# A two-block network in one program: modulation dot products of 1024 rows, all of the first layer's in the first block, loaded from a queue and a pool of their own

## The chip, the core and the metric

One core of a Trainium2 chip runs one program. TensorE (PE in the profile, its weight loads PEld) multiplies matrices, VectorE (DVE) and ScalarE (ACT) work elementwise, GpSimd (POOL) does small chores and issues some DMAs, SyncE (SP) issues most DMAs. Each engine runs its own list of instructions in the order written and waits at semaphores. The metric is the device time of one execution in microseconds (us), median of several runs.

## The reference

Two networks follow each other. The first is one block on a 256 x 2048 input: a norm, a projection to 12288 columns, three branches (multi-window pooling, a 31-tap causal convolution with a layer norm, a short gated convolution), gates, an output projection, and a gated feed-forward layer with a 3-tap convolution. The second has two layers with three kinds of attention over 256 latent and 256 context tokens, and each layer is modulated by a vector:

```
shift, scale, gate       = split(silu(c)     @ w_ada[l] + b_ada[l], 3)
shift_c, scale_c, gate_c = split(silu(c_ctx) @ w_ada[l] + b_ada[l], 3)
h  = rms(x,  norm_w[l]) * (1 + scale)   + shift
hc = rms(xc, norm_w[l]) * (1 + scale_c) + shift_c
...
x  = x + gate * merge_out(...)
xc = xc + gate_c * merge_out(...)      # not in the last layer
```

`w_ada[l]` is 2048 x 6144. Shift and scale are needed where a layer begins, the gates only at its output projection.

## The kernel before

**Weights.** Every product of two f32 matrices is done in three matmuls on split operands (high x high, high x low, low x high). A weight chunk of eight 128 x 128 tiles (512 KB) is loaded by SP into `raw`, ACT rounds it to `wh` (L187), DVE subtracts to get `wl` (L188), and PE runs 24 matmuls of 256 columns on it (L215, L216 on `wh`, then L218 on `wl`). `raw`, `wh` and `wl` have three buffers each, so PE stalls when ACT or DVE falls more than that behind. `w` (L178) records these steps at a priority 400 instructions ahead.

**Order.** A scheduling layer takes the recorded instructions by priority and readiness and writes each engine's list; a list is then fixed. The names in the trace follow the program: `xs`, `hid`, `xsc` are split inputs, `mm` and `st` are PSUM banks.

**Modulation.** It is done on DVE beside the weights, not on PE. For each group of 128 output columns (48 groups) and each of the two vectors, one dot instruction (L400) multiplies a `rawm` tile (128 columns x 512 rows of `w_ada`, transposed) with `crow` (the vector's 512 values, broadcast to all partitions), and accumulates into `mod`. Four passes over 512 rows give 48 x 2 x 4 = 384 dots for the first layer; the second needs 320, since its context gates are unused. One `rawm` load (512 KB) holds two groups, so four dots. `rawm` has two buffers in the weights' pool, and the load for the next four dots is recorded just before the present four. Before each load POOL copies one element (`mark`, L386) that depends on the newest `wl`, so that the load is not issued long before its turn; SP issues the load (L387).

**When.** The dots are tasks with a cost. `earn` (L198) credits the time of the matmuls just recorded times a rate, and runs tasks while there is credit; `spend` takes away other DVE work. The rate is 0.88 in the first block; 0.53, 0.45 and 0.4 in the first layer of the second block; 0.3, 0.3 and 0.5 in the second. In the first block the tasks of the 31-tap convolution come first (`urgent`), then shift and scale of the first layer (256 dots), then its gates (128 dots), as far as the credit goes; what is left of the gates goes on in the second block, before the second layer's dots. At output 8 of the 16 of the last projection (`fdn`, weights `raw<-in_fdn`, L630 to L649) shift and scale must be complete, and from there `ctx_in` (L693) runs: it loads the context in four pieces `xc` into the `rawm` buffers, sums squares (`acc`, L345), makes the norm, loads the pieces again, and makes `xsc` by 16 `h` (L690) and 16 splits (L352). The second block's first products (the `z` gates, weights `in_wz`) read `xsc`. `lat_in` (L715) then stores the four pieces of `x` (`xo<-x`, POOL) and makes `xl`. `norm_conv` (L652) normalises the convolution in four steps at outputs 2, 4, 6 and 7 of the gate loop.

Of the kernel before, what the change touches and what calls it, by code (L numbers as in the profile page):

```python
# [8 lines left out]
F32 = mybir.dt.float32  # L9
# [12 lines left out]
RATES = ((0.53, 0.45, 0.4), (0.3, 0.3, 0.5))  # L22
T = 256
D = 2048
# [50 lines left out]
def lay_out(i):  # L75
# [23 lines left out]
    o["wada"] = two(lambda l: i["w_ada_2"][l].reshape(4, 512, 24, 2, 128).transpose(2, 0, 4, 3, 1))  # L99
# [53 lines left out]
class Net:  # L153
    def __init__(self, tc, aps):
        self.tc, self.nc, self.a = tc, tc.nc, aps
        self.tasks, self.urgent = [], []
        self.credit, self.rate = 0.0, 0.0
        self.ahead = 400
# [131 lines left out]
    def small(self, n, name, bufs=2):  # L290
        return self.st.tile([128, n], F32, name=name, tag=f"s_{name}{n}", bufs=bufs)
# [77 lines left out]


    def modulation(self, l, parts, last):

        nc = self.nc
        mod = self.cr.tile([128, 2, 48], F32, name="mod", tag=f"mod{l}", bufs=1)
        crow, raws = [None], []

        def rows(q):
            c = self.cr.tile([128, 2, 512], F32, name="crow", tag="crow", bufs=1)
            src = self.silu
            nc.sync.dma_start(c, bass.AP(tensor=src.tensor, offset=src.offset + q * 512,  # L380
                                         ap=[[0, 128], [D, 2], [1, 512]]))
# [8 lines left out]
        def pair(q, j, follow):  # L390
            if follow:
                load(*follow)
            raw = raws.pop(0)
            for s in range(2):
                for v in range(2):
                    if last and v and 2 * j + s >= 32:
                        continue
                    junk = self.cr.tile([128, 512], BF16, name="junk", tag="junk", bufs=1)
                    m = mod[:, v, 2 * j + s:2 * j + s + 1]
                    nc.vector.tensor_tensor_reduce(  # L400
                        out=junk, in0=raw[:, s * 512:(s + 1) * 512], in1=crow[0][:, v], op0=OP.mult, op1=OP.add,
                        scale=1.0, scalar=self.col("bada", 2 * j + s, l) if q == 0 else m, accum_out=m)

        lists = []
        for js in ((0, 16), (16, 24)):
            order = [(q, j) for q in range(4) for j in range(*js)]
            tasks = [(0.0, lambda at=order[0]: load(*at))]
            for (q, j), follow in zip(order, order[1:] + [None]):
                if j == js[0]:
                    tasks.append((0.0, lambda q=q: rows(q)))  # L410
                tasks.append((1.4 if last and j >= 16 else 2.7, lambda q=q, j=j, follow=follow: pair(q, j, follow)))
            lists.append(tasks)
        return mod, lists
# [11 lines left out]
    def block1(self):  # L425
# [50 lines left out]
        for j in range(8):  # L476
            pv = proj_in(8 + j)
            pg = proj_in(16 + j)
            if j == 0:
                acc = self.tmp(name="acc")  # L480
                for k in range(16):
                    self.sumsq(acc, x[k], k == 0)
                R = self.rnorm_rows(acc, D, "R1")
                nc.gpsimd.tensor_copy(self.vec2[:, 0, :1], self.mark)
                nc.scalar.dma_start(self.vec2, a["vec2"].rearrange("l p c -> p l c"))
                nc.scalar.dma_start(self.icnt, a["icnt"].rearrange("p (g c) -> p g c", g=4))
                self.silu_rows()
                self.rate = 0.88
# [17 lines left out]
        pooled = self.big.tile([128, 4096], F32, name="pooled", tag="slot", bufs=5)[:, :12 * (8 + T)]  # L506
        pooled = pooled.rearrange("p (b j t) -> p b j t", b=6, j=2)
        nc.gpsimd.memset(pooled[:, :, :, :8], 0.0)
        for g in range(4):
# [7 lines left out]
            for _ in range(g + 1):  # L517
# [5 lines left out]
                                    in1=self.icnt[:, g, None, :w - 1].to_broadcast([128, 2, w - 1]), op=OP.mult)  # L523
# [28 lines left out]
        for f in range(16):  # L552
# [10 lines left out]
            if f in (2, 4, 6, 7):  # L563
                next(norm, None)
                self.spend(4)
# [66 lines left out]
        for f in range(16):  # L632
# [19 lines left out]
    def norm_conv(self, v, c):  # L652

        nc = self.nc
        lsum = self.tmp()
        nc.vector.tensor_reduce(lsum, c.rearrange("p k t -> p t k"), axis=AX.X, op=OP.add)
# [5 lines left out]
        nc.vector.tensor_tensor(out=c, in0=c, in1=mean[:, None, :].to_broadcast([128, 8, T]), op=OP.subtract)  # L662
        nc.scalar.activation(v, c, AF.Square)
        nc.vector.tensor_reduce(lsum, v.rearrange("p k t -> p t k"), axis=AX.X, op=OP.add)
        yield
        r = self.rnorm(lsum, 1024)
        yield
        RL = self.to_rows(r, "RL")
        nc.vector.tensor_tensor(out=c, in0=c, in1=RL[:, None, :].to_broadcast([128, 8, T]), op=OP.mult)
# [23 lines left out]
    def ctx_in(self, xsc):  # L693
# [3 lines left out]
        def piece(q):  # L697
            t = self.wp.tile([128, 1024], F32, name="xc", tag="rawm", bufs=2).rearrange("p (k t) -> p k t", t=T)
# [394 lines left out]
    def proj_c(self, l):  # L1093
# [14 lines left out]
        for name, j0, n, vec, nt in (("ckv", 6, 4, "kvan", 4), ("cq", 0, 6, "qan", nq)):  # L1108
            acc = self.tmp(512, "acc")
            tiles = []  # L1110
            for j in range(n):
                ps = self.bank()
                for k0 in (0, 8):
# [10 lines left out]
                    self.earn(1.28 * nt)  # L1124
# [358 lines left out]
    def modulation_tasks(self, l):  # L1483
        self.mod[l], lists = self.modulation(l, None, l == 1)
        return lists


def net_kernel(tc, aps, stage=2):
# [5 lines left out]
    with contextlib.ExitStack() as es:  # L1494
# [9 lines left out]
        n.cr.tile([128, 16], F32, name="pad", tag="pad")  # L1504
# [11 lines left out]
        n.icnt = n.px.tile([128, 4, 16], F32, name="icnt")  # L1516
        with contextlib.ExitStack() as e2:
            n.big, n.sm, n.ht = (pool(e2, x, side="right") for x in ("big", "sm1", "ht"))
# [4 lines left out]
            n.left = len(deferred)  # L1523
            n.tasks += deferred
            x, acc, n.xc = n.block1()
        n.xlp, n.sm = (pool(es, x, **right) for x in ("xl", "sm2"))
# [35 lines left out]
```

## Time and profile before

| | us |
|---|---|
| median of 3 runs (lowest, highest) | 3245.82 (3238.53, 3248.12) |
| the profiled execution | 3237.02 |
| its span, first to last instruction | 3235.2 |
| PE busy | 3144.7 (97%) |
| DVE busy | 2493.5 (77%) |
| ACT busy | 1541.8 (48%) |
| POOL busy | 131.1 (4%) |

A busy share is a mean over the whole span. PE's is near the whole, so what another engine does counts only where PE waits for it. An engine's idle time is charged to what ended it.

### The profile page before, as it was taken

How to read it: one execution, taken by the hardware profiler on the slowest of the kernel's cores; microseconds unless marked ns; L12 is line 12 of the kernel's file. 1: busy time of each engine (PE TensorE's matmuls, PEld its weight loads, DVE VectorE, ACT ScalarE, POOL GpSimd, SP SyncE). 2: the span in 40 equal slices, each digit the busy share in tenths (PEclk: the TensorE clock that was granted, in tenths of full speed). 3: DMA queues.
4: the chain of work that ended last, by engine and by line, in shares of the span. 5: the costliest groups of instructions: out<-in, count | busy, mean ns of one | idle time of the engine just before them, and what ended most of it. 6: DMA issues, size and time to landing. Idle time of an engine off the chain costs nothing. (4 is left out here: it accounts for less than half of the span.)

```text
span 3235.2 us, 64395 instructions
## 1 busy us (share of the span) xinstructions
PE 3144.7 (97%) x25390; PEld 3097.1 (96%) x25390; DVE 2493.5 (77%) x5285; ACT 1541.8 (48%) x2579; POOL 131.1 (4%) x328
## 2 busy tenths in 40 slices
PE   8999999999999999989999999999999999999999
PEld 8999999999999999989999999999999999999999
DVE  8889977877888888767677888789768776764764
ACT  5444444444554555435444545335545453553553
POOL 0000000000000000000000000000011001000010
PEclk9999999999999999999999999999999999999999
DMA  6556666666666666777654445555477755443456
GB/s 215 182 184 196 205 225 218 225 223 218 218 222 202 228 214 219 232 225 244 186 166 156 140 136 184 190 169 168 154 221 260 229 180 183 136 132 119 128 181 196
DMA packets 190079, 623.16 MB, mean 193 GB/s; under 512 B 21936, under 2 KB 33936, under 8 KB 189776
## 3 DMA queue, kind: packets, MB, share of 16 engines
q1 hardware_dynamic: 180896, 591.75, 56.2%
q0 software_dynamic: 8176, 26.78, 2.5%
q8 instruction: 199, 3.26, 0.4%
q14 instruction: 104, 0.85, 0.1%
q10 hardware_dynamic: 704, 0.52, 0.1%
HBM read 600.33 MB, written 18.63 MB: 191 GB/s over the span
## 5 line engine op out<-in xcount | busy, mean ns | idle before, releaser
L187 ACT ACTIVATE wh<-raw 128x1024 fp32r<-128x1024 f32 (+4 forms) x930 | 940.0, 1013 | 1012.9 <-PE mm L216 283.6
L188 DVE TENSOR_TENSOR wl<-raw,wh 128x1024 fp32r<-128x1024 f32 (+4 forms) x930 | 1081.5, 1164 | 336.5 <-ACT wh L187 320.5
L215 PE MATMUL mm<-xs,wh 128*128 128x256 f32 x2912 | 698.7, 281 | 10.1 <-ACT wh L187 9.8
L216 PE MATMUL mm<-xs,wh 128*128 128x256 f32 x2912 | 697.8, 280 | 2.1 <-DVE xs L355 2.1
L215 PEld LDWEIGHTS mm<-xs,wh 128*128 128x128 f32 x2912 | 550.9, 189 | 11.0 <-ACT wh L187 10.5
L216 PEld LDWEIGHTS mm<-xs,wh 128*128 128x128 f32 x2912 | 551.2, 189 | 2.9 <-DVE xs L355 2.9
L400 DVE CUSTOM_DVE_ANT_0 junk<-rawm,crow,mod 128x512 bf16<-128x512 f32 x528 | 395.5, 749 | 163.9 <-DMA rawm<-in_wada 128.3
L218 PE MATMUL mm<-xs,wl 128*128 128x256 f32 x2912 | 400.3, 280 | 11.9 <-DVE wl L188 11.9
L218 PEld LDWEIGHTS mm<-xs,wl 128*128 128x128 f32 x2912 | 366.0, 189 | 14.1 <-DVE wl L188 13.9
L215 PE MATMUL mm<-hid,wh 128*128 128x256 f32 x688 | 168.1, 284 | 3.4 <-ACT wh L187 3.3
L224 PE MATMUL mm<-wh,xl 128*128 128x384 f32 (+3 forms) x512 | 168.9, 336 | 0.0
L216 PE MATMUL mm<-hid,wh 128*128 128x256 f32 x688 | 167.4, 283 | 0.0
L400 DVE CUSTOM_DVE_ANT_0 junk<-rawm,crow,vec 128x512 bf16<-128x512 f32 x176 | 131.8, 749 | 43.0 <-DMA rawm<-in_wada 40.6
L225 PE MATMUL mm<-wh,xl 128*128 128x384 f32 (+3 forms) x512 | 164.5, 327 | 0.0
L1122 PE MATMUL mm<-xl,wh 128*128 128x256 f32 x640 | 147.6, 279 | 0.0
L215 PEld LDWEIGHTS mm<-hid,wh 128*128 128x128 f32 x688 | 132.8, 193 | 4.2 <-ACT wh L187 4.2
L216 PEld LDWEIGHTS mm<-hid,wh 128*128 128x128 f32 x688 | 133.0, 193 | 0.0
L386 POOL COPY rawm<-wl 128x1 f32<-128x1 f32 x192 | 51.2, 268 | 1944.9 <-DVE wl L188 1534.9
L215 PE MATMUL mm<-xl,wh 128*128 128x256 f32 x512 | 126.2, 286 | 0.0
L215 PE MATMUL mm<-ys,wh 128*128 128x256 f32 x512 | 123.8, 285 | 0.0
L227 PE MATMUL mm<-wl,xl 128*128 128x384 f32 (+3 forms) x512 | 123.4, 327 | 0.0
L216 PE MATMUL mm<-xl,wh 128*128 128x256 f32 x512 | 122.9, 280 | 0.0
(370 smaller groups left out, 6879.6 us busy)
## 6 DMA issues: line engine op xcount, KB each, us to landing
raw<-in_w1in SPq DMA_DIRECT2D x192, 512.0 KB, 4.2
rawm<-in_wada SPq DMA_DIRECT2D x192, 512.0 KB, 5.0
raw<-in_fup SPq DMA_DIRECT2D x172, 512.0 KB, 4.5
raw<-in_wz SPq DMA_DIRECT2D x96, 512.0 KB, 4.1
raw<-in_wout SPq DMA_DIRECT2D x96, 512.0 KB, 4.8
raw<-in_fdn SPq DMA_DIRECT2D x80, 512.0 KB, 4.6
raw<-in_proj SPq DMA_DIRECT2D x48, 512.0 KB, 4.2
raw<-in_wcq SPq DMA_DIRECT2D x40, 512.0 KB, 4.0
```

What stands on the lines that cost most here:

```text
L187: nc.scalar.activation(wh, raw, AF.Copy)
L188: nc.vector.tensor_tensor(out=wl, in0=raw, in1=wh.bitcast(F32), op=OP.subtract)
L215: mm(ps, wh, h, start=first and i == 0, stop=False)
L216: mm(ps, wh, l, start=False, stop=False)
L218: mm(ps, wl, h, start=False, stop=last and i == len(parts) - 1)
L224: mm(ps, h, wh, start=first and i == 0, stop=False)
L225: mm(ps, l, wh, start=False, stop=False)
L227: mm(ps, h, wl, start=False, stop=last and i == len(parts) - 1)
L386: nc.gpsimd.tensor_copy(raw[:, :1], self.mark)
L400: nc.vector.tensor_tensor_reduce(out=junk, in0=raw[:, s * 512:(s + 1) * 512], in1=crow[0][:, v], op0=OP.mult, op1=OP.add, scale=1.0, scala ...
L1122: nc.tensor.matmul(ps[:, s * T:(s + 1) * T], wp, x, start=first and s == 0, stop=k == 15 and m == 2, skip_group_check=True)
```

## The change

- `w_ada` is laid out for dots of up to 1024 rows. The pool for `rawm`, `crow` and `junk` is now its own: 1024 wide in the first block (two `rawm` buffers), 512 wide in the second (four). One `rawm` load of 512 KB holds one group of 1024 rows, so two dots; in the second block a load of 256 KB holds one group of 512 rows, two dots.
- All 192 dots of the first layer (96 groups and passes, two vectors) are tasks of the first block; `later` at output 8 of `fdn` runs all that are left. The second block has the second layer's 320 dots of 512 rows alone.
- The loads of `rawm` and `crow` are issued by POOL, not SP. POOL's `mark` copy stands only before the first loads of a list; later loads wait for their buffer alone. The next load is recorded after the dots.
- Rates are 0.84, 0.36 and 0.3/0.3/0.5. A task of 6.0 us that does nothing stands behind each `crow` load. `proj_c` earns nothing after its last output.
- `ctx_in` takes its `xc` pieces from the new pool's `rawm` buffers.
- `norm_conv` adds by a tree of three adds, works in halves, and is spread over outputs 3 to 8. `icnt` moves into an unused end of a tile, small tiles of `rsqrt` share three buffers, and a pad grows from 16 to 64.

```
-RATES = ((0.53, 0.45, 0.4), (0.3, 0.3, 0.5))
+RATES = ((0.36, 0.36, 0.36), (0.3, 0.3, 0.5))
...
+    def mod_tile(self, name):
+        return self.mp.tile([128, self.wide], F32, name=name, tag="rawm", bufs=8192 // (4 * self.wide))
...
         def rows(q):
-            c = self.cr.tile([128, 2, 512], F32, name="crow", tag="crow", bufs=1)
+            c = mp.tile([128, 2, wide], F32, name="crow", tag="crow", bufs=1)
...
-            nc.sync.dma_start(c, ...
+            nc.gpsimd.dma_start(c, ...
...
-        def load(q, j):
-            raw = self.wp.tile([128, 1024], F32, name="rawm", tag="rawm", bufs=2)
-            nc.gpsimd.tensor_copy(raw[:, :1], self.mark)
-            nc.sync.dma_start(raw.rearrange("p (k c) -> p k c", c=512), self.a["wada"][l, j, q])
+        def load(q, f, wait=False):
+            raw = self.mod_tile("rawm")
+            if wait:
+                nc.gpsimd.tensor_copy(raw[:, :1], self.mark)
+            at = q * wide % 1024
+            nc.gpsimd.dma_start(raw, self.a["wada"][l, q * wide // 1024, f][:, at:at + wide])
...
+        lists, ahead = [], 2048 // wide - 1
+        for fs in ((0, 32), (32, 48)):
+            order = [(q, f) for q in range(D // wide) for f in range(*fs)]
+            tasks = [(0.0, lambda at=at: load(*at, wait=True)) for at in order[:ahead]]
+            for (q, f), follow in zip(order, order[ahead:] + [None] * ahead):
+                if f == fs[0]:
+                    tasks += [(0.0, lambda q=q: rows(q)), (6.0, lambda: None)]
+                cost = (0.23 + wide / 960) * (1 if last and f >= 32 else 2)
+                tasks.append((cost, lambda q=q, f=f, follow=follow: dots(q, f, follow)))
...
             if f == 8:
-                self.later(len(self.tasks) - self.left)
+                self.later(len(self.tasks))
...
-            t = self.wp.tile([128, 1024], F32, name="xc", tag="rawm", bufs=2).rearrange("p (k t) -> p k t", t=T)
+            t = self.mod_tile("xc").rearrange("p (k t) -> p k t", t=T)
...
-                    self.earn(1.28 * nt)
+                    if j < n - 1:
+                        self.earn(1.28 * nt)
```

The first place is DVE's list in the gate loop of the first block, some 480 us in (`gate`, `m` and `brb` belong to that loop, `junk` is a dot's unused product, a row `mod` reads the sum). Before:

```order
L188 TENSOR_TENSOR wl<-raw,wh 128x1024
L400 ISA junk,mod<-rawm,crow,mod 128x512
L400 ISA mod 128x1
L400 ISA junk,mod<-rawm,crow,mod 128x512
L400 ISA mod 128x1
L591 TENSOR_TENSOR gate<-mm,gate 128x256
L188 TENSOR_TENSOR wl<-raw,wh 128x1024
```

And now:

```order
L189 TENSOR_TENSOR wl<-raw,wh 128x1024
L361 TENSOR_TENSOR brb<-tmp,brb 128x256
L403 ISA junk,mod<-rawm,crow,vec_81 128x1024
L403 ISA mod 128x1
L189 TENSOR_TENSOR wl<-raw,wh 128x1024
L467 TENSOR_TENSOR gate<-mm,R_344 128x256
L403 ISA junk,mod<-rawm,crow,vec_81 128x1024
L403 ISA mod 128x1
L189 TENSOR_TENSOR wl<-raw,wh 128x1024
```

A wide dot now stands behind nearly every `wl`. Before, 114 dots of 512 rows stand between the 135th and the 260th of the 930 `wl`; now 127 dots of 1024 rows stand there, one more up to the 507th, and 49 from there to the 548th, which is the last `wl` of `fdn`.

The second place is DVE's list around the context's norm and `xsc`. Before, it stands between the `wl` of `fdn`'s outputs 10 to 13:

```order
L188 TENSOR_TENSOR wl<-raw,wh 128x1024
L345 TENSOR_TENSOR acc<-acc,sq 128x256 x2
L690 SCALAR_TENSOR_TENSOR h<-xc,gain,Rc 128x256 x3
L188 TENSOR_TENSOR wl<-raw,wh 128x1024
L352 SCALAR_TENSOR_TENSOR xsc<-h,mod,xsc 128x256 x3
L690 SCALAR_TENSOR_TENSOR h<-xc,gain,Rc 128x256
L188 TENSOR_TENSOR wl<-raw,wh 128x1024
```

Now the end of the last dots and the beginning of the context's sums read:

```order
L403 ISA junk,mod<-rawm,crow,mod 128x1024
L403 ISA mod 128x1
L348 TENSOR_TENSOR acc<-acc,sq 128x256 x19
L303 TENSOR_SCALAR rsv<-st 128x2
L348 TENSOR_TENSOR acc<-acc,sq 128x256
```

These rows stand behind the last `wl` of `fdn`, behind the three `wl` of the next products, and behind the addition of `fdn`'s last output to `x`. Between that addition and the sums stand 12 dots, and the next `wl` comes after 12 of the 16 `h` and 8 of the 16 `xsc`.

The third place is POOL's list, with what each row waits for (PE and Activation stand for semaphores of those engines, DVE for VectorE's, DMASW for a DMA that POOL issued), near the end of the first layer's loads. Now:

```order
L395 DMA rawm<-in_wada 128x1024 [waits DMASW0_49,DVE_49]
L386 DMA crow<-silu 128x2x512 [waits PE_49,Activation_49]
L395 DMA rawm<-in_wada 128x1024 [waits DMASW1_49,DVE_49]
L395 DMA rawm<-in_wada 128x1024 [waits DMASW2_49,DVE_49]
L755 DMA xo<-x 128x1024 [waits DMAHW0_49,DVE_49]
L395 DMA rawm<-in_wada 128x1024 [waits DMASW4_49,DVE_49]
L395 DMA rawm<-in_wada 128x1024 [waits DMASW5_49,DVE_49]
L395 DMA rawm<-in_wada 128x1024 [waits DMASW7_49,DVE_49]
L395 DMA rawm<-in_wada 128x1024 [waits DMASW0_49,DVE_49]
```

The row `crow` of 2 x 512 is the second layer's first one. It is written where a `hid` tile of the first block lies, and the PE semaphore that it waits for is that of the last matmul of `fdn` on that tile. Six of the first layer's loads stand behind it. Before, POOL's list there held only `mark` copies, `xo` and `bias`.

## Rows read from the trace of the kernel before

**Rows 1.** The page, part 1: busy us, share, count.

```profile
PE 3144.7 (97%) x25390; PEld 3097.1 (96%) x25390; DVE 2493.5 (77%) x5285; ACT 1541.8 (48%) x2579; POOL 131.1 (4%) x328
```

**Rows 2.** Waits of PE, whole span: total us, times, longest.

```profile
PE mm L218 <- DVE wl L188: 26.0, 22, 3.4
```

**Rows 3.** Waits of DVE, whole span.

```profile
DVE junk L400 <- DMA rawm<-in_wada: 169.0, 106, 4.8
DVE junk L400 <- DMA crow<-silu: 21.5, 7, 5.8
```

**Rows 4.** Timeline of DVE near 1378 us: start, us, instruction, idle before it.

```profile
1377.30 0.75 DVE L400 CUSTOM_DVE_ANT_0 junk<-rawm,crow,vec 128x512 bf16<-128x512 f32 x1 [2.75 <-DMA rawm<-in_wada]
...
1380.37 2.35 DVE L188 TENSOR_TENSOR wl<-raw,wh 128x1024 fp32r<-128x1024 f32 x2
```

**Rows 5.** Stretches: length; PE, PEld, DVE, ACT, POOL busy (count); clock; DMA.

```profile
376.00:742.00 366.00, 352.47 (x2997) 349.03 (x2997) 288.40 (x517) 169.48 (x216) 6.64 (x27) 1.00 0.66 221
742.00:1450.00 708.00, 690.72 (x5826) 687.20 (x5826) 576.97 (x1042) 341.24 (x463) 14.64 (x50) 0.99 0.66 219
1450.00:1560.00 110.00, 106.79 (x914) 106.00 (x914) 78.04 (x137) 59.32 (x91) 1.05 (x2) 0.98 0.74 237
...
1625.00:2033.00 408.00, 399.47 (x2825) 388.30 (x2824) 335.49 (x912) 201.36 (x488) 27.80 (x69) 1.00 0.49 158
2033.00:2283.00 250.00, 241.11 (x1951) 235.80 (x1950) 209.59 (x537) 100.90 (x185) 10.77 (x36) 0.99 0.55 175
...
2571.00:2694.00 123.00, 117.48 (x810) 115.04 (x809) 92.11 (x236) 56.62 (x113) 7.47 (x23) 0.99 0.57 185
2694.00:3235.20 541.20, 529.49 (x4159) 513.74 (x4157) 334.08 (x834) 261.30 (x511) 27.77 (x55) 0.99 0.48 154
```

**Rows 6.** The dots of L400 alone in such stretches: DVE busy (two instructions each).

```profile
376.00:742.00 366.00, 86.35 (x228) 1.00 0.66 221
...
1450.00:1560.00 110.00, 3.51 (x10) 0.98 0.74 237
1625.00:2033.00 408.00, 147.38 (x390) 1.00 0.49 158
2033.00:2283.00 250.00, 97.59 (x257) 0.99 0.55 175
2571.00:2694.00 123.00, 21.20 (x56) 0.99 0.57 185
```

**Rows 7.** DVE by form, whole span: count, busy us, mean ns, idle before.

```profile
L188 DVE TENSOR_TENSOR wl<-raw,wh 128x1024 fp32r<-128x1024 f32 x776 | 947.6, 1222 | 265.7 <-ACT wh L187 254.1 <-PE at L364 5.7 <-PE mm L218 1.5
...
L345 DVE TENSOR_TENSOR acc<-acc,sq 128x256 f32<-128x256 f32 x105 | 42.7, 420 | 3.5 <-ACT sq L344 2.3
...
L352 DVE SCALAR_TENSOR_TENSOR xsc<-h,mod,xsc 128x256 fp32r<-128x256 f32 x16 | 7.0, 478 | 0.0
L690 DVE SCALAR_TENSOR_TENSOR h<-xc,gain,Rc 128x256 f32<-128x256 f32 x16 | 6.9, 478 | 0.0
```

**Rows 8.** Windows at DVE's densest and in PE's two paces, and under a fallen clock.

```profile
50.00:100.00 50.00, 50.00 (x427) 50.00 (x427) 48.64 (x87) 21.74 (x25) 0.50 (x2) 1.00 0.56 183
250.00:300.00 50.00, 50.00 (x443) 50.00 (x443) 44.97 (x78) 23.41 (x28) 0.56 (x2) 1.00 0.62 199
362.03:365.44 3.41, 3.41 (x18) 3.41 (x17) 3.38 (x8) 1.87 (x3) 0.00 (x0) 0.50 0.80 263
```

**Rows 9.** DMA issues: queue, count, KB each, median us to landing.

```profile
rawm<-in_wada SPq DMA_DIRECT2D x192, 512.0 KB, 5.0
...
crow<-silu SPq DMA_DIRECT2D x16, 512.0 KB, 6.1
...
xc<-in_ctxT SPq DMA_DIRECT2D x8, 512.0 KB, 4.9
...
x<-xn POOLq DMA_DIRECT2D x4, 512.0 KB, 6.8
```

More of the change, by code (lines that the diff above doesn't have):

```diff
@@ L97, in lay_out @@
     two = lambda f: np.stack([f(l) for l in range(2)])
-    o["wada"] = two(lambda l: i["w_ada_2"][l].reshape(4, 512, 24, 2, 128).transpose(2, 0, 4, 3, 1))
+    o["wada"] = two(lambda l: i["w_ada_2"][l].reshape(2, 1024, 48, 128).transpose(0, 2, 3, 1))
     def vec2(l):
@@ L368, in later, with modulation @@
             self.tasks.pop(0)[1]()
-    def modulation(self, l, parts, last):
-        nc = self.nc
+    def mod_tile(self, name):
+        return self.mp.tile([128, self.wide], F32, name=name, tag="rawm", bufs=8192 // (4 * self.wide))
+    def modulation(self, l, last):
+        nc, wide, mp = self.nc, self.wide, self.mp
         mod = self.cr.tile([128, 2, 48], F32, name="mod", tag=f"mod{l}", bufs=1)
@@ L391, in pair, with dots @@
+        def dots(q, f, follow):
+            raw = raws.pop(0)
+            for v in range(1 if last and f >= 32 else 2):
+                junk = mp.tile([128, wide], BF16, name="junk", tag="junk", bufs=1)
+                m = mod[:, v, f:f + 1]
+                nc.vector.tensor_tensor_reduce(
+                    out=junk, in0=raw, in1=crow[0][:, v], op0=OP.mult, op1=OP.add,
+                    scale=1.0, scalar=self.col("bada", f, l) if q == 0 else m, accum_out=m)
             if follow:
                 load(*follow)
-            raw = raws.pop(0)
@@ L394, in pair @@
[L394 to L411, printed above, removed]
+        lists, ahead = [], 2048 // wide - 1
@@ L654, in norm_conv, with total @@
         nc = self.nc
-        lsum = self.tmp()
-        nc.vector.tensor_reduce(lsum, c.rearrange("p k t -> p t k"), axis=AX.X, op=OP.add)
+        half = (slice(0, 4), slice(4, 8))
+        wide = lambda row: row[:, None, :].to_broadcast([128, 4, T])
+        def total(x):
+            out = self.tmp()
+            for o, n in ((v[:, :4], 4), (v[:, :2], 2), (out, 1)):
+                lo, hi = (x[:, 0], x[:, 1]) if n == 1 else (x[:, :n], x[:, n:2 * n])
+                nc.vector.tensor_tensor(out=o, in0=lo, in1=hi, op=OP.add)
+                x = v
+            return out
+        lsum = total(c)
         yield
@@ L661, in norm_conv @@
         nc.scalar.mul(mean, mps[:, :T], 1.0 / 1024)
-        nc.vector.tensor_tensor(out=c, in0=c, in1=mean[:, None, :].to_broadcast([128, 8, T]), op=OP.subtract)
-        nc.scalar.activation(v, c, AF.Square)
-        nc.vector.tensor_reduce(lsum, v.rearrange("p k t -> p t k"), axis=AX.X, op=OP.add)
+        for h in half:
+            nc.vector.tensor_tensor(out=c[:, h], in0=c[:, h], in1=wide(mean), op=OP.subtract)
+            nc.scalar.activation(v[:, h], c[:, h], AF.Square)
+        yield
+        lsum = total(v)
         yield
@@ L668, in norm_conv @@
         RL = self.to_rows(r, "RL")
-        nc.vector.tensor_tensor(out=c, in0=c, in1=RL[:, None, :].to_broadcast([128, 8, T]), op=OP.mult)
+        for h in half:
+            nc.vector.tensor_tensor(out=c[:, h], in0=c[:, h], in1=wide(RL), op=OP.mult)
+            yield
     def conv3(self, o, u, name, n, j):
@@ L1522, in net_kernel @@
             n.tasks, deferred = n.modulation_tasks(0)
-            n.left = len(deferred)
             n.tasks += deferred
             x, acc, n.xc = n.block1()
-        n.xlp, n.sm = (pool(es, x, **right) for x in ("xl", "sm2"))
+        n.wide = 512
+        n.xlp, n.sm, n.mp = (pool(es, x, **right) for x in ("xl", "sm2", "mp2"))
         n.pp = pool(es, "pp2", space=PSUM, reuse_waits="tile")
```

30 lines of the change are left out of this document (16 added, 14 removed).

## The prediction

> **What bounds the kernel now.** I read the page's busy shares first, then the waits, then DVE's timeline around one of them, then busy time by stretch. TensorE is busy 3144.7 of 3235.2 us [rows 1], so 90.5 us of idle is nearly all there is to win, and every wait that the change adds to PE is paid in full. Within that, 26.0 us in 22 waits are late `wl` [rows 2]. The cause is seen on DVE: its dots wait 169.0 us for `rawm` and 21.5 us for `crow` [rows 3], and the next two `wl` stand behind such a dot, which came 2.75 us late [rows 4]. DVE is 77% busy as a mean, but the mean hides the stretches, and the change has to be costed in them [rows 5]. A gap also costs after it ends: at 362 us the clock stood at 0.50, the 1.2 GHz level, for 3.41 us, and PE did 18 matmuls where its usual pace of 113 to 117 ns gives 30 [rows 8]: 12 x 0.115, some 1.4 us.
>
> **Size of a dot.** A 512-row dot is 86.35 us / 114 = 0.757 us with its readout [rows 6]. DVE's slope follows from two widths of a two-input f32 subtraction and addition: (1222 - 420) / 768 = 1.04 ns per element [rows 7]. So 1024 rows take 0.757 + 512 x 0.00104 = 1.29 us, 0.22 us less than two of 512. If the longer product is not slower per element, that is the price; the bounds are 1.22 (a `wl`) and 1.51 (two short dots).
>
> **Stretch 376 to 742 us** (gate loop up to `fdn`'s forerunners). DVE did 288.4 us, 86.35 of it dots [rows 5, 6]. Instead of 114 short ones 127 long ones stand there: 288.4 - 86.35 + 127 x 1.29 = 365.9 us in a stretch of 366. With some 97%, the densest that DVE ran while PE waited for nothing [rows 8], this needs 377 us: +11. In the middle `crow` is replaced; a load of twice the 6.1 us load's bytes [rows 9] starts after the last dot of the old rows, and what the 6.0 us of rest does not cover holds the `wl` behind it. I take 4 us, so +15 for the stretch. Bounds: +1 if DVE fills its time wholly and `crow` is in time; +30 with dots of 1.33 us and a full `crow` wait. The rebuilt `norm_conv` exchanges reductions for additions; I put it at 0, between -5 and +5, since the row nearest to its pieces is 420 ns for 256 elements [rows 7].
>
> **742 to 1450 us.** One dot is left. PE's idle there is 708.0 - 690.7 = 17.3 us [rows 5], of which waits at `rawm` and the slow clock behind them are the greater part. I take -18 (idle and clock), bounds -8 and -22.
>
> **1450 to 1560 us** (`fdn`'s last outputs). DVE did 78.0 us, of it 3.5 dots [rows 5, 6]. The context's sums, `h` and `xsc` leave: 16 x 0.42 + 32 x 0.478 [rows 7] and about 1.6 for the norm, 23.6 us. 49 long dots come, 63.2 us. Sum 114.1; at 97% 117.6 us in place of 110: +8, and +4 for the next replacement of `crow`, so +12 (bounds 4 and 18).
>
> **The boundary between the blocks** is the largest term. Before, the context was normalised beside `fdn`'s outputs 10 to 13, so `xsc` was ready when the `z` gates began. Now `later` runs all 40 remaining tasks there, `ctx_in` takes its pieces from the same two `rawm` buffers, and so stands after the last dot. In addition the second layer's `crow` stands in POOL's list ahead of the last six loads, and waits for PE's last `fdn` matmul. So 12 dots begin when `fdn` has ended, and PE has only the first weights of the `z` gates, whose products need `xsc`. The chain: 12 dots in pairs of 2.6 us whose loads come two at a time; three rounds of 2.6 + 5.0 to 6.8 [rows 9] are 23 to 28 us; two rounds of `xc` pieces, 2 x (4.9 [rows 9] + 1.6) = 13; the norm and its way over three engines, 3.5; 16 `h` and 16 `xsc`, 32 x 0.478 = 15.3 [rows 7]. Together 55 to 60, less 5 us of the context norm's other products on PE that can fill it, and 1.7 for the clock behind the gap: +52. The lower bound is DVE's own busy time: 12 x 1.29 + 16 x 0.42 + 2 + 15.3 = 39.5 us, less 5, plus the first load's landing of 5: +39. The upper is 60.
>
> **1625 to 2033 us.** 195 short dots become 256 of the same width: 335.5 - 147.4 + 256 x 0.757 = 381.9 us of 408 [rows 5, 6], 94%. Loads are half as large and three ahead, but `crow` is replaced four times, and between them DVE has 26 us to spare where its waits took more. I take +15, bounds 0 and +40.
>
> **2033 to 2283 us.** 97.6 us of dots go [rows 6], and with them most of PE's 8.9 idle us: -8 (bounds -2, -10). **2571 to 2694 us:** 64 dots for 28, 92.1 - 21.2 + 48.4 = 119.3 of 123 us [rows 5, 6]: +2 (bounds -3, +8). **2694 us to the end:** no dots; PE's idle is 541.2 - 529.5 = 11.7 [rows 5], half of it behind other waits: -6 (bounds 0, -9). **The first dots**, near 360 us, no longer cut PE off for 2.5 us and slow its clock [rows 8]: -3 (bounds -4, 0).
>
> **Sum.** 15 - 18 + 12 + 52 + 15 - 8 + 2 - 6 - 3 = +61, on 3237.0 us of the profiled execution: 3298. That execution lies 8.8 us under the median, 3245.8, and by it the sum is 3307. I forecast 3302.
>
> **POOL's queue.** The loads go from SP to POOL. Here the x pieces from POOL landed after 6.8 us, `rawm` of the same 512 KB from SP after 5.0 [rows 9]. Two buffers hide a landing L while two dots at one per `wl` take longer: the two buffers turn over in L + 2.6 us + 1.5 for the `wl` between them, for two pairs of 2.9 us each on average (366 us / 127 x 2 = 5.8 per pair). So L up to 7.5 costs nothing in the first block.
>
> The Trainium skill, "SBUF — State Buffer", section "SBUF: two separate sides", says that descriptors of a DMA issued by GpSimd are written by GpSimd's own cores, and are held up while VectorE keeps the shared port in one of its two-port modes. No row of before shows whether dots or `wl` do so; the 6.8 against 5.0 us agrees with it in sign. By that rule the loads would come late in DVE's densest stretches, which is the second rival below.
>
> **The rivals.** *First: faster, since DVE's order fits PE's.* Mechanism: DVE at 97% held PE up nowhere in 50 to 100 us [rows 8]; if its dots, with loads in time, fill only slack, then PE's idle goes everywhere but at the boundary. The idle of the stretches is 13.5 + 17.3 + 8.5 + 8.9 + 5.5 + 11.7 = 65.4 [rows 5], and taking four fifths of it and the slow clock's 5 us gives -57; the boundary at its lower bound costs +39, 1450 to 1560 us +4: -14, 3232 us. It decides as soon as the waits between dots and `wl` in 376 to 742 and 1625 to 2033 us stay under some 10 us in total. Against it: 365.9 us of work in 366, where 50 to 100 us had 97%, and the boundary, which no order on DVE can hide, since PE's next product needs `xsc`. Between it and the forecast lies the case of no change: the boundary at 39 to 45 and the other stretches' losses at 0 to 10, 3236 to 3256.
>
> *Second: POOL's loads land late.* If L is 10 us, two pairs need 14.1 us where 11.6 are there: 1.2 us for each of 63 pairs, +76 in the first stretch in place of +15, of which some is made up by the three buffers of weights; with the boundary's three rounds 10 longer I take +45 over the forecast: 3347 us. For it speaks 6.8 against 5.0, against it that 6.8 is still hidden.
>
> *Third: PE's pace.* Matmuls take 112.9 ns in some windows and 117.1 in others with PE never idle [rows 8]. If stages change from one to the other, a stretch like 742 to 1450 with 5826 matmuls moves by 5826 x 0.0042 = 24 us, either way. I can't predict it, and widen the range by 20.
>
> **How the numbers follow.** Forecast 0.72: 3302, its own range 3262 to 3340. Late loads 0.13: 3347. The faster rival 0.08: 3232. No change 0.07. The pace lies on top of each. The range from 3253 to 3352 leaves out the faster case, the most of no change and the top of the late loads. About 10 us (0.3%, 3236 to 3256) is what a measurement of this kernel can tell from no change: faster 0.08, same 0.07, slower 0.85.
>
> **What would show it.** Right: one gap of PE of about 50 us where `fdn` ends, ended by `xsc` or `h`, with the `crow` issue on POOL waiting for PE, and six loads behind it; DVE over 97% busy in the gate loop and hardly a PE wait for `wl` between 742 and 1450 us; dots of 1.29 us. Wrong: a boundary gap under 20 us, or dots whose waits for `rawm` grow past 169 us in total (the late loads), or PE idle that falls in the gate loop as well (the faster rival).

## The result, and the profile after

The changed kernel took 3289.89 us (median of 4 runs, 3279.89 to 3291.75) beside 3246.49 for the kernel before: a ratio of 1.0135, 95% interval [1.0112, 1.0158]. Slower by 43 us was measured where 56 were forecast; the time lies within the stated range. The profiled execution took 3291.75 us, 54.7 more than that of before, where the sum had +61.

Part 1 of the page after, to be read beside [rows 1], and PE's waits, summed over the span with times and longest, beside [rows 2]:

```profile
PE 3143.1 (96%) x25390; PEld 3096.6 (94%) x25390; DVE 2452.0 (75%) x4907; ACT 1552.7 (47%) x2580; POOL 242.1 (7%) x444
```

```profile
PE st L317 <- DVE acc L348: 46.2, 2, 45.2
PE mm L219 <- DVE wl L189: 22.2, 11, 4.2
```

PE is as busy as before, within 2 us; the 54.8 us by which the span grew are idle time. One wait, for the context's sums, is 45.2 of them. Late `wl` cost about what they did (22.2 for 26.0). DVE's list around that wait (start, us, instruction, idle before it):

```profile
1548.20 0.42 DVE L642 TENSOR_TENSOR x<-x,mm 128x256 f32<-128x256 f32 x1
1552.46 1.28 DVE L403 CUSTOM_DVE_ANT_0 junk<-rawm,crow,mod 128x1024 bf16<-128x1024 f32 x1 [3.84 <-DMA rawm<-in_wada]
...
1560.69 0.42 DVE L642 TENSOR_TENSOR x<-x,mm 128x256 f32<-128x256 f32 x1
1563.76 1.28 DVE L403 CUSTOM_DVE_ANT_0 junk<-rawm,crow,mod 128x1024 bf16<-128x1024 f32 x1 [2.65 <-DMA rawm<-in_wada]
...
1582.26 1.28 DVE L403 CUSTOM_DVE_ANT_0 junk<-rawm,crow,mod 128x1024 bf16<-128x1024 f32 x1
...
1584.44 1.48 DVE L348 TENSOR_TENSOR acc<-acc,sq 128x256 f32<-128x256 f32 x3 [0.89 <-ACT sq L347]
...
1601.22 1.28 DVE L712 SCALAR_TENSOR_TENSOR h<-xc,gain,Rc 128x256 f32<-128x256 f32 x3 [1.78 <-ACT Rc L329]
1602.41 1.27 DVE L355 SCALAR_TENSOR_TENSOR xsc<-h,mod,xsc 128x256 fp32r<-128x256 f32 x3
```

PE's last `fdn` matmul starts at 1550.1 us. Dots run until 1583.6, sums until 1597, the norm until 1601, and the first `z` matmul starts at 1602.3. The stretches after (length; PE, PEld, DVE, ACT, POOL busy; granted clock; DMA), the gate loop, the up projection, the boundary, the `z` gates after it, and the stretch with the second layer's gates:

```profile
380.00:723.00 343.00, 327.30 (x2761) 324.35 (x2760) 325.43 (x504) 154.86 (x194) 30.86 (x58) 0.99 0.79 263
...
816.00:1286.00 470.00, 470.00 (x4146) 470.00 (x4145) 344.58 (x527) 259.34 (x346) 0.00 (x0) 1.00 0.60 194
...
1550.00:1602.00 52.00, 2.59 (x12) 2.07 (x10) 36.88 (x90) 10.20 (x26) 4.39 (x8) 0.54 0.63 202
1602.00:1646.00 44.00, 41.38 (x306) 40.49 (x307) 38.01 (x88) 26.89 (x52) 1.18 (x2) 0.88 0.51 160
...
2520.00:2904.00 384.00, 361.31 (x2643) 352.74 (x2642) 259.50 (x634) 176.27 (x352) 50.08 (x94) 0.98 0.55 172
```

The same places of the kernel before, cut by the same matmuls:

```profile
375.00:713.00 338.00, 326.12 (x2770) 322.88 (x2769) 264.45 (x474) 155.01 (x195) 6.45 (x26) 0.99 0.66 222
...
806.00:1298.00 492.00, 487.84 (x4139) 486.79 (x4138) 418.78 (x751) 253.44 (x348) 8.35 (x28) 1.00 0.66 217
...
2484.00:2848.00 364.00, 354.59 (x2638) 346.72 (x2638) 259.92 (x634) 176.91 (x350) 20.21 (x56) 0.99 0.56 181
```

Lengths between the same first or last matmuls of a tile (a last one is the last on `wh`), before and after:

| stretch | before | after | change |
|---|---|---|---|
| start to first gate product (`bra`) | 295.3 | 302.9 | +7.6 |
| to the last `ms` product | 509.7 | 512.7 | +3.0 |
| up projection | 492.9 | 470.2 | -22.7 |
| `fdn` to its last matmul | 261.1 | 264.0 | +2.9 |
| boundary, to the first `xsc` product | 1.5 | 52.5 | +51.0 |
| first `z` gates | 34.7 | 42.7 | +8.0 |
| first layer up to the first `xl` of its out-projections | 445.5 | 444.1 | -1.4 |
| to the first `xc` product | 443.0 | 430.8 | -12.2 |
| second layer up to its last `xl` product | 364.6 | 383.9 | +19.3 |
| to the last matmul | 383.3 | 382.6 | -0.7 |

### The profile page after: what moved, and what is told of

Read it like the earlier page. It is cut to its first block, busy times and chain, and to the rows that moved or that the text cites. A ratio compares the mean times of both kernels' runs of the same rounds, so it can differ in the third digit from the quotient of the medians.

```text
span 3290.0 us, 63924 instructions
## 1 busy us (share of the span) xinstructions
PE 3143.1 (96%) x25390; PEld 3096.6 (94%) x25390; DVE 2452.0 (75%) x4907; ACT 1552.7 (47%) x2580; POOL 242.1 (7%) x444
## 3 DMA queue, kind: packets, MB, share of 16 engines
q1 hardware_dynamic: 148896, 482.69, 45.2%
## 5 line engine op out<-in xcount | busy, mean ns | idle before, releaser
L403 DVE CUSTOM_DVE_ANT_0 junk<-rawm,crow,mod 128x512 bf16<-128x512 f32 (+1 forms) x336 | 303.1, 902 | 55.0 <-DMA crow<-silu 25.5
L395 POOL DMA_DIRECT2D rawm<-in_wada x288 | 154.3, 536 | 860.8 <-DVE mod L403 675.7
L403 DVE CUSTOM_DVE_ANT_0 junk<-rawm,crow,vec 128x1024 bf16<-128x1024 f32 (+1 forms) x176 | 183.3, 1041 | 33.8 <-DMA rawm<-in_wada 33.0
```

The source lines that it names most:

```text
L395: nc.gpsimd.dma_start(raw, self.a["wada"][l, q * wide // 1024, f][:, at:at + wide])
L403: nc.vector.tensor_tensor_reduce(out=junk, in0=raw, in1=crow[0][:, v], op0=OP.mult, op1=OP.add, scale=1.0, scalar=self.col("bada", f, l) i ...
```

## The experiments

Each ran beside the kernel before on its own chip. Chips differ by 0.7% (3246 us for the kernel before in the result above, 3219 to 3224 in these), so ratios are compared. A ratio without its interval is one that was given before.

**1. The context first** (`left` is the number of the gates' tasks).

```
             if f == 8:
-                self.later(len(self.tasks))
+                self.later(len(self.tasks) - self.left)
...
             if f == 11:
                 self.run(ctx)
-                self.spend(10)
+                self.later(len(self.tasks))
```

> The changed kernel, but the tasks of the first layer's gates are recorded behind the context's norm and xsc instead of ahead of them. Theory (the gap at the boundary comes from the order: xsc stands behind the last dots, and the two rawm buffers are shared): xsc is ready before fdn ends, the 45 us gap of PE at 1595 us falls under 10, and the 46 dots that now stand beside the z gates slow these by 10 to 25 us; 3250 to 3270 us in all. Rival (the gap comes from something else there, such as the weights or POOL's queue): a gap over 30 us stays, and the time is within 10 us of 3290.

Measured: 3269.89 us, 1.0140 [1.0105, 1.0176], as slow as the change. By the time the rival was right (its 3280 to 3300 us are ratios of 1.010 to 1.017), but neither of its causes was seen. `xsc` was ready in time, and the gap came back in three pieces of 13.2, 6.5 and 34.3 us. The last two stretches of it, and the last one again with DVE's dots alone:

```profile
1572.00:1588.00 16.00, 9.55 (x41) 9.22 (x41) 13.21 (x24) 3.40 (x6) 1.62 (x4) 0.68 0.68 229
1588.00:1623.00 35.00, 0.73 (x4) 0.44 (x3) 34.02 (x67) 6.67 (x14) 5.40 (x10) 0.56 0.37 128
```

```profile
1588.00:1623.00 35.00, 24.19 (x38) 0.56 0.37 128
```

DVE works for 34.0 of 35 us, 24.2 of them dots, while PE waits for its first product on `xl`. The `xl` splits stand among these dots, and so does the `z` addition (L1333) with which the wait ends in the profile. So the theory fell in its narrow form: it matters little where `xsc` stands among the dots; the dots left over there are what PE waits behind.

**2. POOL's queue freed of the wait for PE.**

```
+            queue = nc.sync if l and not q else nc.gpsimd
-            nc.gpsimd.dma_start(c, bass.AP(...
+            queue.dma_start(c, bass.AP(...
```

> The changed kernel, but the second layer's first crow load is issued by SyncE, so that POOL's last loads of the first layer do not stand behind its wait for the last fdn matmul. Theory (order and two buffers make the gap; POOL waited for PE only 0.8 us there): the gap stays at 40 to 47 us, the time at 3285 to 3295. Rival, as the prediction had it (the queued loads start the last dots late): the gap falls by 10 to 20 us, the time to 3270 to 3280.

Measured: 3274.91 us, 1.0162 [1.0131, 1.0194]. PE's longest wait is the same to 0.1 us:

```profile
PE st L317 <- DVE acc L348: 47.4, 2, 45.2
```

The `crow` in POOL's list delayed nothing. After the change it had waited for PE for 0.8 us, and the loads behind it for their buffers (POOL, 1545 to 1590 us):

```profile
POOL rawm L395 <- DVE mod L403: 23.4, 6, 5.7
...
POOL crow L386 <- PE mm L219: 0.8, 1, 0.8
```

**3. The flush alone, on the kernel before.**

```
             if f == 8:
-                self.later(len(self.tasks) - self.left)
+                self.later(len(self.tasks))
```

> The kernel before with one edit: at output 8 of fdn all tasks that are left run, the gates of the first layer too. Narrow dots, SyncE's loads and the old pool stay. Theory (the order alone makes the gap): xsc stands behind fdn's last addition here too, but no dots stand there; a gap of 25 to 35 us at the boundary, part of it given back by a lighter second block, 3262 to 3285 us. Rival (the wide dots and the new queue are needed for the loss): a gap under 10 us, 3235 to 3250 us. On the pace of matmuls: the projection between 810 and 1300 us has its dots here, and if the dots set the pace its matmuls take 117 to 118 ns; if not, any value between 113 and 118.

Measured: 3246.07 us, 1.0073 [1.0047, 1.0099], within the theory's ratios (1.005 to 1.012). From `fdn`'s last product on `wh` to the first on `xsc` it is 14.8 us, with 4.8 and 5.0 us of waits for the sums and the norm in it. That lies between the theory's gap of 25 to 35 and the rival's of under 10: no dot stands there, and PE starts with the first `xsc`. In the up projection the pace changed from 118 to 113 ns at 1035 us with dots on both sides.

**4. The gates back in the second block, 512 rows wide.**

```
-RATES = ((0.36, 0.36, 0.36), (0.3, 0.3, 0.5))
+RATES = ((0.53, 0.45, 0.4), (0.3, 0.3, 0.5))
...
-            n.tasks += deferred
...
+        n.tasks += n.modulation(0, False, n.mod[0])[1][1]
         lat = n.lat_in(x, acc)
```

> The changed kernel, but the first layer's gates are left out of the first block: their 128 dots are recorded for the second block, 512 rows wide, at the rates of before (0.53, 0.45, 0.4). Wide dots, own pool and POOL's queue stay. Theory (what is lost is the boundary, what is gained is the stretch from 742 to 1300 us without dots): no gap at the boundary, matmuls at 113 to 114 ns between 816 and 1286 us, and a second block as before or up to 15 us longer for its denser dots: 3220 to 3245 us. Rival (the wide dots or POOL's queue cost by themselves): 3255 to 3275 us.

Measured: 3233.16 us, 1.0035 [1.0020, 1.0051]. The boundary is gone (0.4 us), and from 823 to 1274 us 3981 matmuls took 451.0 us, 113.3 ns each. But the second block, from the first `wh,xsc` product to the last matmul, took 1684 us, 48 more than before's 1636, not the 15 expected: with 180 dots between 2055 and 2331 us, PE waited up to 8.6 us for sums that stood behind them. By the ratio the theory (0.992 to 1.000) missed and the rival (1.003 to 1.009) held; its cause, that wide dots or POOL's queue cost by themselves, doesn't follow, since what is regained at the boundary is in part lost again where the same dots go, 512 rows wide.

**5. Credit for all the gates.**

```
-                self.rate = 0.84
+                self.rate = 0.94
```

> The changed kernel with one number: the first block's rate is 0.94, not 0.84. All tasks of the first layer are then recorded before output 8 of fdn, where 40 were left; 64 wide dots stand between the 350th and 450th wl (in the first block's up projection) and none in fdn, and the context's norm and xsc stand beside fdn's outputs 10 to 13 again. Theory (the loss is the 40 tasks that the credit leaves for the boundary): no gap at the boundary, 45 to 60 us less than the changed kernel, a ratio to the kernel before of 0.993 to 1.001. Rival (the wide dots cost PE as much wherever they stand, as the first experiment's moved gaps suggest): the 64 dots make gaps in the up projection of 30 us or more, ratio over 1.006.

Measured: 3235.18 us, 1.0026 [1.0003, 1.0050], beside 1.0135 for the change. The boundary is 0.5 us. With 64 wide dots in it, the up projection took 489 us for 470. PE's idle there is 7.2 us, of which 4.4 in one wait, and the rest is its slower pace, so the rival's gaps of 30 us did not come. The cause of the boundary is the credit: at 0.84, 40 tasks were left at output 8 of `fdn`; at 0.94, none. The gain is about 35 us by the ratios, less than the 45 to 60 expected, and the theory's 0.993 to 1.001 was missed.

**6 to 8. POOL's mark before every load.** In all blocks (6), at rate 0.94 in the second block (7), at rate 0.94 in both (8). The first edit is that of 6 and 8, the second that of 7.

```
-        def load(q, f, wait=False):
+        def load(q, f, wait=True):
...
-                load(*follow)
+                load(*follow, wait=wide == 512)
```

> The changed kernel with POOL's mark copy before every rawm load, as in the kernel before, so that loads and dots come where they are recorded: 75 wide dots go from the gate loop into the up projection, 62 gate dots of the second layer spread over 18 and 46, and its other dots over 107, 74 and 74. The 40 tasks left at output 8 of fdn stay. Theory: the boundary gap stays (40 to 55 us); the stretch between 2480 and 2850 us gets back most of the 19 us that it lost to bunched gate dots; the gate loop gains up to 10 us; ratio 1.004 to 1.011. Rival (POOL's copies before each load delay the dots and these the wl, as in the kernel before): ratio 1.012 or more. On the pace of matmuls, if dots in the up projection slow them, 117 to 118 ns there; else 113 to 114 in part.

> Rate 0.94 as in the experiment before, and a mark copy before each load of the second block alone. Theory: no gap at the boundary, and the stretch with the second layer's first dots to its gates some 10 to 20 us shorter than with rate 0.94 alone: ratio 0.988 to 0.997. Rival (bunched gate dots are not what costs there): within 0.2% of rate 0.94 alone.

> Rate 0.94 and a mark copy before every load, in both blocks: 68 dots in the gate loop in place of 101, 110 in the up projection. Theory: gate loop up to 8 us shorter, up projection 5 to 15 us longer by waits of dots for loads in front of wl and PE's slower pace: within 0.3% of the experiment with marks in the second block alone. Rival (dense dots in the gate loop cost more than spread ones): 0.4% or more faster than it.

Measured: 3540.50, 3381.00 and 3604.66 us; ratios 1.0985 [1.0942, 1.1028], 1.0492 [1.0458, 1.0527], 1.1174 [1.1133, 1.1215]. All three theories fell, and so did the rivals of 7 and 8; the rival of 6 had the direction, not the size. Experiment 6, POOL and then DVE around one load, and DVE's waits:

```profile
501.58 0.18 POOL L393 COPY rawm<-wl 128x1 f32<-128x1 f32 x1 [9.70 <-DVE wl L189]
502.09 0.53 POOL L395 DMA_DIRECT2D rawm<-in_wada  x1 [0.32 <-POOL rawm L393]
```

```profile
501.77 1.22 DVE L189 TENSOR_TENSOR wl<-raw,wh 128x1024 fp32r<-128x1024 f32 x1
509.88 1.29 DVE L403 CUSTOM_DVE_ANT_0 junk<-rawm,crow,vec 128x1024 bf16<-128x1024 f32 x1 [6.90 <-DMA rawm<-in_wada]
```

```profile
DVE junk L403 <- DMA rawm<-in_wada: 611.6, 217, 7.3
```

The load starts when its `wl` is done, one `wl` ahead of its dot, and the dot waits for the whole transfer: 217 waits of 2.8 us, 611.6 against 57 after the change and 169.0 in [rows 3]. Before, a `rawm` load was recorded ahead of the four dots that ran meanwhile; here it stands behind its two. With a load recorded behind its dots, marks before every load cost 5 to 11% here (7 and 8 beside 5, 6 beside the change). Marks with a load recorded ahead of the dots, as before, were not tried in this layout.

**9 and 10. A few marks.** At rate 0.94, before every fourth load of the second layer's gates (9); also before every sixteenth load of the first block (10); the edit of 9:

```
-                load(*follow)
+                load(*follow, wait=last and follow[1] >= 32 and follow[1] % 4 == 0)
```

> Rate 0.94, and in the second layer's gates alone a mark copy before every fourth load, with three loads in flight. Of their 64 dots 17 then stand between the 777th and 810th wl, 43 between the 810th and 860th, where rate 0.94 alone has 62 and 2. Theory (the stretch around 2660 us is longer because bunched dots stand in front of khl, qs and the context's sums on DVE): its idle falls by 10 us or more, and the time by 10 to 18 us against rate 0.94 alone, a ratio to the kernel before of 0.997 to 1.000. Rival (the loads behind marks land late, as in the experiments with marks before every load): 1.004 or more.

> The experiment before, and in the first block a mark copy before every sixteenth load: 69 wide dots stand between the 135th and 260th wl in place of 101, and 96 in the up projection in place of 64. Theory (dense wide dots and crow waits make the gaps of some 18 us in the gate loop of rate 0.94): 5 to 12 us less than the experiment before, ratio 0.994 to 0.998. Rival (what is taken from the gate loop comes back in the up projection): the same within 0.2%.

Measured: 3231.14 us, 1.0026 [1.0007, 1.0045], and 3227.11 us, 1.0026 [1.0004, 1.0049], both no different from 5, so the theory of 9 (0.997 to 1.000) and its rival (1.004 or more) both missed. The stretch to the last `xl` and the last stretch, in 9 and then in 5:

```profile
2462.00:2833.00 371.00, 357.25 (x2644) 349.59 (x2644) 244.07 (x586) 176.32 (x351) 37.88 (x78) 0.98 0.49 159
2833.00:3228.00 395.00, 382.46 (x3084) 371.26 (x3082) 245.92 (x594) 187.36 (x339) 30.65 (x55) 0.98 0.51 166
```

```profile
2473.00:2858.00 385.00, 363.45 (x2641) 354.15 (x2640) 258.63 (x634) 175.72 (x350) 50.20 (x94) 0.97 0.53 171
2858.00:3242.00 384.00, 379.62 (x3084) 369.12 (x3083) 230.80 (x546) 187.78 (x340) 15.96 (x24) 1.00 0.46 153
```

The bunched dots did cost 14 us in the first, and 11 came back in the last, where the dots went. In 10's profile the stretch to the last `ms` product was 504 us for 512 in 9. The time is the same within 0.2%, so the rival held by its number; its cause did not show, since the up projection was no longer either (484 us for 486).

**11. Narrow dots in the first block**, the context in eight pieces.

```
-        self.wide = 1024
+        self.wide = 512
...
-                self.rate = 0.84
+                self.rate = 1.00
...
-                    tasks += [(0.0, lambda q=q: rows(q)), (6.0, lambda: None)]
+                    tasks += [(0.0, lambda q=q: rows(q)), (3.0, lambda: None)]
```

> The changed kernel with dots of 512 rows in the first block too: four rawm buffers of 256 KB, three loads ahead, crow loads of 512 KB with a rest of 3.0, the context in eight pieces, and rate 1.00, so that no task is left at output 8 of fdn. 256 narrow dots stand before the 260th wl and 128 between the 260th and 450th, 43 us more of DVE work than 192 wide ones (384 x 0.757 less 192 x 1.29 us). Theory (DVE is full in the gate loop): 10 to 30 us slower than rate 0.94, ratio 1.005 to 1.012. Rival (the width is worth nothing, since loads three ahead hide the rest): within 0.2% of 1.0026.

Measured: 3244.11 us, 1.0080 [1.0055, 1.0104]: 0.54% above the wide dots of 5, within the theory's ratios. The theory's place for it isn't borne out. In the profiles of 11 and then of 5, the stretch from the first `bra` product to the last `ms` one, in which the gate loop lies, is the shorter with narrow dots:

```profile
310.00:824.00 514.00, 494.50 (x4181) 489.07 (x4181) 453.87 (x891) 238.98 (x299) 65.78 (x121) 0.99 0.75 245
```

```profile
303.00:824.00 521.00, 498.60 (x4178) 495.73 (x4177) 445.09 (x676) 238.81 (x299) 35.55 (x67) 0.98 0.72 247
```

The profile of 11 even spans less, 3237.6 us for 3246.1; but 5's profiled execution was the slowest of its 12 and 11's the second fastest of its 7. The rate, the number of loads and the pieces of the context changed with the width. So the medians speak for the wide dots; where they gain isn't shown.

**12. The loads through SyncE.** Rate 0.94; the first loads of a list keep their mark, as after the change.

```
-            nc.gpsimd.dma_start(c, bass.AP(...
+            nc.sync.dma_start(c, bass.AP(...
...
-            nc.gpsimd.dma_start(raw, self.a["wada"]...
+            nc.sync.dma_start(raw, self.a["wada"]...
```

> Rate 0.94 with the rawm and crow loads issued by SyncE again, without marks. Theory (a load that waits for its rawm buffer holds back the weight loads behind it in SyncE's list): waits of wh for raw rise, 15 to 60 us slower than rate 0.94, ratio 1.007 to 1.02. Rival (three raw buffers hide that, and SyncE's loads land sooner): within 0.2% of 1.0026 or less.

Measured: 3197.21 us, 0.9920 [0.9888, 0.9951]: faster than the kernel before and 1.06% under 5. The theory fell and the rival held, with more than it asked. Page after, DVE's waits, and the landing of loads (in 5, then in 12):

```profile
PE 3131.4 (98%) x25390; PEld 3085.7 (96%) x25390; DVE 2438.9 (76%) x4907; ACT 1550.6 (48%) x2580; POOL 80.2 (3%) x144
```

```profile
DVE junk L403 <- DMA rawm<-in_wada: 35.1, 28, 3.9
DVE junk L403 <- DMA crow<-silu: 23.1, 7, 5.8
...
DMA to landing us min/median/max: 2.9/3.8/11.7
```

```profile
DVE junk L403 <- DMA crow<-silu: 17.7, 8, 3.0
DVE junk L403 <- DMA rawm<-in_wada: 12.4, 13, 2.3
...
DMA to landing us min/median/max: 2.6/3.9/7.3
```

The medians agree, the tail doesn't: counted in the two traces, 12 of the 96 wide loads took over 7 us by POOL, 1 by SyncE. Dots waited 30.1 us in place of 58.2. PE's idle fell from 91.0 to 66.6 us (span less busy), and PE itself was busy 23.7 us less for the same matmuls (its two paces are shown in the last section). So about half of the 48 us between these two profiles is PE's busy time, and 5's profile is the slowest of its 12 executions, 3247.90 us beside a median of 3235.18.

The tail explains a part of the waits at most. Of the 35.1 us for `rawm` in 5, 7.8 stood behind wide loads of over 7 us, 9.6 behind other wide ones, and 17.7 behind the 256 KB loads of the second block. Nor did POOL's list hold the loads up: of the 94 wide loads that reuse a buffer, 90 were issued 0.3 us after the last dot on it (0.04 by SyncE). Why these loads take longer at times stays open. In the kernel before, where SyncE issued them, 18 of 192 took over 7 us too, so the queue alone doesn't decide it. The lists changed as well: DVE's has 59 dots between the 777th and 810th `wl` in 12, 62 in 5.

## Why the prediction was right

**The boundary** was the largest term and came out: +51.0 for +52. That it fits to 1 us is luck, since its parts were off in both directions, and 52 was the low end of its own chain (55 to 60, less 5, plus 1.7). The 12 dots took 22.4 us (1561.1 to 1583.5; 23 to 28 were reckoned from two buffers), but they began 11 us after PE's last `fdn` matmul. The addition of `fdn`'s last output stood behind four more dots, one of which waited 3.84 us for its load, and three `wl`. `xsc` then took 19, not 32, since PE starts with the first of 16. The first `z` gates became 8 us longer, a term put at 1.7: in their first 10 us PE did 50 matmuls at a granted clock of 0.66, where before it did 90 at 1.00, and it waited 1.9 us for a norm. The statement that POOL's `crow` holds the last dots back was wrong: it waited 0.8 us, and experiment 2 without it has the same gap. The sum did not need it. Experiment 1 corrects the picture further: with `xsc` made early, the same dots hold up `xl` and `z`. Experiment 5 shows the root, which the prediction took as given: too small a rate leaves 40 tasks there.

**A dot of 1024 rows** was put at 1.29 us with its readout. In the gate loop (380 to 723 us) 229 instructions, 114.5 dots, took 148.2 us, 1.29 each. For the sign of the width there are the medians of experiment 11 alone.

**The other stretches** of the forecast are not those of the table above. Between the matmuls that stand at its bounds in the trace of before, the lengths changed so:

| forecast's stretch, us before | forecast | measured | PE's idle before, after |
|---|---|---|---|
| start to 376 | -3 | +4.8 | 16.4, 14.7 |
| 376 to 742 | +15 | +8.4 | 13.5, 17.9 |
| 742 to 1450 | -18 | -46.2 | 17.3, 1.1 |
| 1450 to the end of `fdn` | +12 | +23.6 | 2.8, 19.2 |
| boundary | +52 | +51.0 | 0.9, 49.7 |
| from there to 1625 | 0 | +8.1 | 0.2, 2.4 |
| 1625 to 2033 | +15 | -0.3 | 8.5, 7.0 |
| 2033 to 2283 | -8 | -12.1 | 8.9, 1.0 |
| 2283 to 2571 | 0 | +1.6 | 4.8, 4.1 |
| 2571 to 2694 | +2 | +22.3 | 5.5, 21.8 |
| 2694 to the end | -6 | -6.6 | 11.7, 8.0 |

Misses of up to 28 us cancel in the sum, so +54.7 for +61 is luck in part. The rows after for 376 to 742, 742 to 1450, 1450 to `fdn`'s end and 2571 to 2694 us (before: [rows 5]), and for the third of them DVE's waits and PE's largest:

```profile
380.90:755.30 374.40, 356.46 (x2998) 352.91 (x2997) 354.81 (x552) 168.62 (x213) 33.49 (x63) 0.98 0.79 263
755.30:1417.20 661.90, 660.79 (x5827) 660.59 (x5826) 456.45 (x674) 351.52 (x465) 3.04 (x6) 1.00 0.62 198
1417.20:1549.80 132.60, 113.45 (x903) 111.27 (x902) 104.53 (x146) 40.33 (x43) 13.94 (x26) 0.94 0.76 249
...
2610.20:2755.50 145.30, 123.46 (x810) 119.98 (x809) 114.49 (x308) 56.13 (x113) 39.31 (x75) 0.94 0.72 228
```

```profile
DVE junk L403 <- DMA rawm<-in_wada: 22.8, 10, 5.5
DVE junk L403 <- DMA crow<-silu: 4.0, 1, 4.0
...
PE mm L219 <- DVE wl L189: 15.1, 7, 4.2
```

**742 to 1450 us.** The waits went as reckoned: PE's idle fell by 16.2 us. The other 30 are PE's busy time, 690.7 us for 5826 matmuls before and 660.8 for 5827 after. This is the third rival's effect, which was reckoned at 24 us either way. In the up projection, most of this stretch, idle fell by only 4.2 us, 492.0 - 487.8. The rest is pace: 487.84 us for 4139 matmuls before, 117.9 ns, and 470.00 for 4146 after, 113.4 ns. Experiment 3, whose lists up to there are those of the kernel before, took 482.5 us for 492.9 in it, so a part of this gain can't be put down to the change. Over the whole span PE's busy time is the same within 2 us: the gain was lost at the start (+6.2 before the first `bra`), in the `z` gates and in the second layer.

**1450 us to the end of `fdn`** was underrated, beyond its bounds (4 and 18). The step that failed is that landings up to 7.5 us cost nothing in the first block. DVE had less to do than reckoned, 104.5 us for 114.1, but its dots waited 22.8 us for loads that landed after 4.8 to 8.3 us, and 4.0 for `crow` as reckoned. The formula took 2.9 us of time for each dot, the mean of the gate loop; here 104.5 us of work hold 48 dots, 2.2 each, and by the same formula only landings up to 4.6 us are hidden (4 x 2.18 - 4.1).

**The gate loop** (376 to 742) was within its bounds. DVE did 354.8 us for 365.9, waited 10.1 for `rawm`, 5.3 for `crow` (4 were reckoned) and 3.1 for `wh`, 373.3 of 374.4 us in all; so it was full, at 95% busy and not over 97%. PE's idle rose by 4.4 us. **1625 to 2033 us** was overrated: DVE did 376.8 us for 381.9, PE lost less than before, and the 15 us set aside for the replacements of `crow` weren't needed; dots waited 6.7 us for them. **2033 to 2283** came near.

**The second layer's gates** (2571 to 2694) were underrated, +22.3 for +2. The sum took DVE's busy time, 119.3 of 123, and not the order: 62 of 64 dots stand between the 777th and 810th `wl`, 26 before, ahead of sums, `khl` and `qs`. PE waited 6.1 us for `qs`, 5.9 for `khl` and 3.5 for sums, and its idle there rose from 5.5 to 21.8 us.

**The rivals.** The faster one failed: PE's idle outside the boundary did not fall in sum (90.5 us before, 146.9 less 49.7 after). Late loads of POOL were kept as a rival at 10 us of landing; the median was 5.3 after the change, for 5.0 in [rows 9], and the waits for `rawm` fell from 169.0 [rows 3] to 57.4, so it did not happen as priced; 22.8 of the 57.4 stand before the end of `fdn`, as told above. With the loads on SyncE the same kernel is 1.06% faster by experiments 5 and 12, which the forecast had at nothing; how much of that is the queue isn't shown. The Trainium skill, "SBUF — State Buffer", section "SBUF: two separate sides", has GpSimd kept from writing a DMA's descriptors while VectorE runs an operation in one of its two-port modes, of which it names an f32 copy. The tail (11.7 against 7.3 us at most) agrees in sign; no run here shows that descriptors are the reason, or that dots or the subtractions for `wl` run in such a mode.

## What to carry to other kernels

Where tasks are run on a credit, count what is left at the point by which all must be done: a rate 0.1 too small here put 40 tasks on the path that ends last, 1.1% of the time. Ask of each load how long before its use it is issued, and by which queue; a mark that ties it to the newest step exposes the whole transfer, and two buffers that hide a landing at a stretch's mean spacing don't where the dots stand closer. Of the parts of this change the rate is shown to be a loss; by the medians the wide dots are a gain and the loads by POOL a loss, and without these two losses it is 0.8% faster than the kernel before. A single profile can differ from another by pace alone, so compare stretches by PE's idle and busy time apart.

## What was not expected of the hardware

PE has two paces on the same 128 x 256 matmuls at a granted clock of 1.00 and without idle time: 113.3 to 113.4 ns and 117.6 to 118 ns, each for hundreds of microseconds. Dots do not set it. In experiment 5 the faster one holds with 15 dots (850 to 1100 us, 113.4 ns) and the slower one without a dot (1280 to 1480 us, 117.6 ns):

```profile
850.00:1100.00 250.00, 249.94 (x2204) 249.65 (x2203) 195.65 (x302) 134.90 (x181) 5.09 (x10) 1.00 0.60 208
...
1280.00:1480.00 200.00, 200.00 (x1701) 200.00 (x1700) 117.06 (x158) 96.36 (x133) 1.08 (x2) 1.00 0.67 209
```

It mostly changes where PE was interrupted, and is worth some 4% of such a stretch. The lists don't decide it either. Those of the kernel before and of experiment 3 are the same on every engine up to 1450 us, and yet PE did 1743 matmuls in one and 1801 in the other, with dots in both (before, then 3):

```profile
1065.00:1270.00 205.00, 205.00 (x1743) 205.00 (x1742) 178.75 (x318) 106.84 (x149) 3.67 (x12) 1.00 0.65 219
```

```profile
1065.00:1270.00 205.00, 204.41 (x1801) 204.02 (x1800) 178.94 (x320) 107.92 (x149) 3.33 (x11) 1.00 0.65 222
```

Experiments 1 and 2, on one chip and with the same lists there, did 443 and 426 from 200 to 250 us. What decides it stays open.
